# Seven block products in four of 22 pairs of the down products, x scaled in the first gate pass, sums ahead of any split

## The chip, the cores and the metric

The kernel runs on one core of one Trainium2 chip. The metric is the device time of one execution in microseconds (us), from start to end on that core. Engines are named as in the profile: PE is TensorE's matmul, PEld its weight load, DVE is VectorE, ACT is ScalarE, POOL is GpSimd, SP is SyncE (here it only issues DMAs).

## The reference

One decoder layer on x of 256 rows and 2048 columns, float32:

```python
x = x + 0.5 * swiglu(rms_norm(x, g1), gate1, up1, down1)      # D_FF = 5632
x = x + mix(rms_norm(x, g2))   # joint projection, RWKV-7 time mixing | RG-LRU, output projection
x = x + 0.5 * swiglu(rms_norm(x, g3), gate2, up2, down2)
out = rms_norm(x, final_norm)

def rms_norm(x, g): return x * rsqrt(mean(x * x, -1) + 1e-6) * g
def swiglu(x, w_gate, w_up, w_down): return (silu(x @ w_gate) * (x @ w_up)) @ w_down
```

## The kernel before

**Splits.** A float32 operand is split into a high part (a cast to fp32r on ACT, `whi`) and a low part (the difference, on DVE, `wlo`). A product of 128 rows by 512 columns over one k tile of 128 is three matmuls: high by high, high by low, low by high. Weights arrive by DMA from SP, 1 MB (two k tiles of 1024 columns, a *pair*) in one transfer, into `wst`; `wst`, `whi` and `wlo` are three rotating buffers each.

**FFN.** `ffn` walks the 5632 hidden columns in a first chunk of 512 and five of 1024. Each chunk has a gate pass and an up pass over the 16 k tiles of x. In the first chunk x is the row-unscaled input: the transposes come before the row norms are known. Its gate pass multiplies as it is; `after_first()` then makes `rstd`, `spread_rstd` (L203 to L206) lays it along the free axis as `rb`, and the silu and `hid` (L351) take `rstd` as a scale. During the up pass of the first chunk `normalised(p)` scales two k tiles of x at a time for all later chunks: add high and low (L279), times `rb` (L280), cast (L281), low part (L282). For the first three pairs it also makes four block sums of x (L286 to L289) and splits them (L291, L292) into `xsums`.

**S pairs.** In the chunks of 1024, a pass is eight pairs by the plan `nSnSnSnn`. An `n` pair is 24 matmuls of 512 columns (two k tiles, two row tiles, two column halves, three products). An `S` pair treats rows, k and columns as 2x2 blocks and makes seven block products instead of eight, so 21 matmuls; for it `pairs` (L107ff) makes three sums of weight blocks on DVE: L125 (1024 columns), L127 and L128 (512 each), and splits b11/b21, b22, t1/t3 and t2/t4. These four splits take four `whi` buffers in turn; an `n` pair takes two. Products that belong to several output blocks gather in four `aux` banks of PSUM, the others in four `own` banks; `shared` (L296 to L304) adds the `aux` banks into `sg` or `hid` after the last S pair, and the loops at L317 and L324 add the `own` banks after the pass.

**Down.** hidden is transposed (`hidden_T`, L263, evicted at L270, L271) into `hThi` and `hTlo`, 44 k tiles. The down product goes through `weights` and `rows_times` (L174, L175, L177): pieces of 1024 columns in FFN1 (two), one of 1024 and two of 512 in FFN2, all with eight products for each pair. L371 adds half of each bank into the residual `h`.

**Order.** The tile scheduler sets each engine's order by priority. Weight loads, splits and sums of a pair are written at a high priority (offset 4000), so they stand ahead of the work around them. Each engine runs its queue in that order. Mix (`Mix`) runs its projections through `columns_times` (L186 to L188), evicts by `rb` into `raw` (L571) and inverts small matrices on DVE (L754, L758, copy L762) at the same time.

Of the kernel before, what the change touches and what calls it, by code (L numbers as in the profile page):

```python
# [21 lines left out]
class Core:
# [80 lines left out]
    def pairs(self, mat, c0, plan):  # L103
# [3 lines left out]
        ns = plan.count("S")  # L107
        ids = {"S": iter(range(ns)), "n": iter(range(ns, self.NK // 2))}
        for kind in plan:
            p = next(ids[kind])  # L110
# [29 lines left out]
    def rows_times_pairs(self, mat, c0, plan, own, aux, xhi, xlo, sums, hooks):  # L140
# [3 lines left out]
        for at, (kind, p, w) in enumerate(self.pairs(mat, c0, plan)):  # L144
# [7 lines left out]
            else:  # L152
                x = lambda k, t: tuple(v[:, 2 * p + k, t * P : (t + 1) * P] for v in (xhi, xlo))
                sm = lambda n: tuple(sums[:, p, h, n * P : (n + 1) * P] for h in range(2))
# [3 lines left out]
                self.three(own[1], sm(3), w["b22"], first, last)  # L158
                self.three(aux[1], sm(0), w["t1"], f, l)
                self.three(aux[3], sm(2), w["t3"], f, l)  # L160
                self.three(aux[2], sm(1), w["t2"], f, l)
# [84 lines left out]
def ffn(core, xhi, xlo, rstd, wg, wu, wd, after_first, after_down, fpool, down, rest, back, head=None):  # L246
# [11 lines left out]
    def hidden_T(c0, w, hid):  # L258
        for j in range(0, w // P, 2):
# [13 lines left out]
            )  # L273

    def normalised(p):

# [6 lines left out]
        if p < NSUM:  # L283
            blk = lambda k, t: tmp[:, k, t * P : (t + 1) * P]
            raw = scrap[:, 1, 512:].rearrange("p (n s) -> p n s", n=4)
            nc.vector.tensor_tensor(raw[:, 0], blk(0, 1), blk(1, 1), ALU.add)  # L286
            nc.vector.tensor_tensor(raw[:, 1], raw[:, 0], blk(0, 0), ALU.subtract)
            nc.vector.tensor_tensor(raw[:, 2], blk(0, 0), blk(0, 1), ALU.subtract)
            nc.vector.tensor_tensor(raw[:, 3], blk(1, 0), raw[:, 1], ALU.subtract)  # L289
            flat = raw.rearrange("p n s -> p (n s)")  # L290
            nc.scalar.copy(sums[:, p, 0, :], flat)  # L291
            nc.vector.tensor_tensor(sums[:, p, 1, :], flat, sums[:, p, 0, :].bitcast(F32), ALU.subtract)  # L292
# [916 lines left out]
```

## Time and profile before

| what | value |
|---|---|
| median of 3 runs | 1953.26 us (1949.84 to 1953.41) |
| the profiled execution | 1948.99 us, of it the span of the trace 1947.3 us |
| granted TensorE clock, mean | 0.994 |
| PE busy | 1907.3 us (98%) |
| DVE busy | 1440.3 us (74%) |
| ACT busy | 985.8 us (51%) |
| DMA | 360.77 MB, mean 185 GB/s |

All durations and starts of rows come from the profiled execution, which was 4.27 us below the median. A matmul's row lasts longer than its turn: matmuls overlap, so the price of one is the distance between starts. A number in brackets at the end of a row is the idle time of the engine just before it, with the instruction that ended it.

### The profile page before, as it was taken

To read this page: it belongs to the slowest core of one execution; us is meant where nothing else is said; L and a number is where in the kernel's file an instruction comes from. 1 tells how busy PE (TensorE), PEld (TensorE's weight loads), DVE (VectorE), ACT (ScalarE), POOL (GpSimd) and SP (SyncE) were. 2 spreads that over 40 slices of the span, in tenths; PEclk is the share of its full clock that TensorE was granted. 3 is DMA by queue.
4 is the path that set the end of the run, shared out by engine and by line. 5 is a ranking of instruction groups with operands and counts; after the bars stand their busy time and mean duration, and the time that the engine had idled before them with its cause. 6 is when DMAs were issued, how large, how long until landed. Compare 5 with 4: busy or idle time off the path is not lost.

```text
span 1947.3 us, 25669 instructions
## 1 busy us (share of the span) xinstructions
PE 1907.3 (98%) x10233; PEld 1589.7 (82%) x10233; DVE 1440.3 (74%) x1822; ACT 985.8 (51%) x1189; POOL 9.9 (1%) x53
## 2 busy tenths in 40 slices
PE   8899999999999999999999999999999999999997
PEld 6678877878888889998899878778888888788886
DVE  5989898888645446876696775899898989844553
ACT  6465555555444335544454555565556555543443
POOL 0000000000000001000000000000000000000000
PEclk9999999999999999999999999999999999999999
DMA  6356555565755556545243456555555655766553
GB/s 238 129 198 214 173 194 195 178 212 190 264 186 204 194 195 207 177 127 163 77 144 115 131 195 215 173 194 182 199 197 198 211 183 184 257 211 193 195 194 129
DMA packets 130032, 360.77 MB, mean 185 GB/s; under 512 B 20879, under 2 KB 23128, under 8 KB 129784
## 3 DMA queue, kind: packets, MB, share of 16 engines
q1 hardware_dynamic: 129592, 358.08, 55.6%
q8 instruction: 80, 1.31, 0.3%
q10 hardware_dynamic: 320, 1.06, 0.1%
q14 instruction: 40, 0.33, 0.0%
HBM read 351.25 MB, written 7.86 MB: 184 GB/s over the span
## 4 chain that ended last, share of the span: by engine, by line
PE 89%; DVE 5%; ACT 3%; issue 2%; DMA 1%; SPq 0%; ACTq 0%; DVEq 0%
PE bank L137 14%; PE bank L136 13%; PE bank L138 13%; PE bank L175 10%; PE bank L177 10%; PE bank L174 10%; PE bank L186 4%; PE bank L188 4%; PE bank L187 4%; ACT whi L99 1%; DVE wlo L82 1%; PE bank L263 1%; DVE wlo L100 1%; PE bank L712 1%; PE bank L640 1%
## 5 line engine op out<-in xcount | busy, mean ns | idle before, releaser
L82 DVE TENSOR_TENSOR wlo<-wst,whi 128x1024 fp32r<-128x1024 f32 (+2 forms) x329 | 398.2, 1212 | 344.6 <-ACT whi L81 343.9
L99 ACT CAST whi<-wst 128x1024 fp32r<-128x1024 f32 (+1 forms) x440 | 430.4, 993 | 364.0 <-PE bank L138 321.9
L81 ACT CAST whi<-wst 128x1024 fp32r<-128x1024 f32 (+2 forms) x329 | 343.2, 1044 | 472.5 <-PE bank L177 335.8
L100 DVE TENSOR_TENSOR wlo<-wst,whi 128x1024 fp32r<-128x1024 f32 (+1 forms) x440 | 493.3, 1147 | 90.9 <-ACT whi L99 85.0
L174 PE MATMUL bank<-whi,hThi 128*128 128x512 f32 x704 | 274.2, 389 | 0.0
L175 PE MATMUL bank<-wlo,hThi 128*128 128x512 f32 x704 | 274.0, 389 | 0.0
L177 PE MATMUL bank<-whi,hTlo 128*128 128x512 f32 x704 | 231.4, 389 | 0.0
L186 PE MATMUL bank<-xahi,whi 128*128 128x256 f32 x688 | 199.1, 290 | 3.2 <-DVE raw L571 3.2
L188 PE MATMUL bank<-xahi,wlo 128*128 128x256 f32 x688 | 197.9, 288 | 0.0
L136 PE MATMUL bank<-whi,xahi 128*128 128x512 f32 x490 | 191.4, 393 | 6.3 <-ACT xahi L281 4.6
L187 PE MATMUL bank<-xalo,whi 128*128 128x256 f32 x688 | 197.3, 287 | 0.0
L137 PE MATMUL bank<-wlo,xahi 128*128 128x512 f32 x490 | 191.5, 391 | 0.6 <-DVE wlo L100 0.6
L136 PE MATMUL bank<-whi,xbhi 128*128 128x512 f32 x490 | 190.2, 391 | 1.9 <-DVE hid L351 1.4
L137 PE MATMUL bank<-wlo,xbhi 128*128 128x512 f32 x490 | 191.1, 390 | 0.6 <-DVE wlo L100 0.6
L138 PE MATMUL bank<-whi,xalo 128*128 128x512 f32 x490 | 191.4, 391 | 0.0
L138 PE MATMUL bank<-whi,xblo 128*128 128x512 f32 x490 | 190.7, 389 | 0.0
L175 PEld LDWEIGHTS bank<-wlo,hThi 128*128 128x128 f32 x704 | 132.2, 188 | 27.4
L177 PEld LDWEIGHTS bank<-whi,hTlo 128*128 128x128 f32 x704 | 132.1, 188 | 27.4
L174 PEld LDWEIGHTS bank<-whi,hThi 128*128 128x128 f32 x704 | 132.2, 188 | 27.1
L186 PEld LDWEIGHTS bank<-xahi,whi 128*128 128x128 f32 x688 | 133.1, 193 | 7.3 <-DVE raw L571 3.6
L188 PEld LDWEIGHTS bank<-xahi,wlo 128*128 128x128 f32 x688 | 132.9, 193 | 1.9 <-issue 1.1
L187 PEld LDWEIGHTS bank<-xalo,whi 128*128 128x128 f32 x688 | 133.1, 194 | 1.2 <-issue 0.2
(298 smaller groups left out, 2557.3 us busy)
## 6 DMA issues: line engine op xcount, KB each, us to landing
wst<-in_ffn_w_up_dram SPq DMA_DIRECT2D x88, 1024.0 KB, 5.0
wst<-in_ffn_w_down_dram SPq DMA_DIRECT2D x88, 1024.0 KB, 4.9
wst<-in_ffn_w_gate_dram SPq DMA_DIRECT2D x87, 1024.0 KB, 5.0
wst<-in_w_in_dram SPq DMA_DIRECT2D x40, 1024.0 KB, 5.0
wst<-in_w_out_dram SPq DMA_DIRECT2D x16, 1024.0 KB, 5.7
h<-parked SPq DMA_DIRECT2D x4, 1024.0 KB, 9.2
wst<-in_w_in_dram SPq DMA_DIRECT2D x4, 640.0 KB, 4.4
h<-in_x_dram SPq DMA_DIRECT2D x4, 512.0 KB, 4.7
```

The lines of the kernel that those rows point to most:

```text
L82: nc.vector.tensor_tensor(lo[:, : m * width], src, hi[:, : m * width].bitcast(F32), ALU.subtract)
L99: self.nc.scalar.copy(hv, src)
L100: self.nc.vector.tensor_tensor(lv, src, hv.bitcast(F32), ALU.subtract)
L136: nc.tensor.matmul(out, a[0], b[0], start=first, stop=False)
L137: nc.tensor.matmul(out, a[0], b[1], start=False, stop=False)
L138: self.last_mm = nc.tensor.matmul(out, a[1], b[0], start=False, stop=last)
L174: nc.tensor.matmul(banks[t][n][:, :w], a, whi[:, c : c + w], start=first, stop=False)
L175: nc.tensor.matmul(banks[t][n][:, :w], a, wlo[:, c : c + w], start=False, stop=False)
L177: self.last_mm = nc.tensor.matmul(banks[t][n][:, :w], b, whi[:, c : c + w], start=False, stop=last)
L186: nc.tensor.matmul(out, a, xhi[:, k, :], start=first, stop=False, skip_group_check=True)
L187: nc.tensor.matmul(out, a, xlo[:, k, :], start=False, stop=False, skip_group_check=True)
L188: nc.tensor.matmul(out, b, xhi[:, k, :], start=False, stop=last, skip_group_check=True)
```

## The change

1. **Down.** Pieces of 1024 columns go through `rows_times_pairs` with 22 pairs, four of them S (the last eight k tiles, at positions 6, 10, 14, 18 of the first piece and 3, 8, 13, 18 of the second; FFN2 has only a first piece). `hidden_T` of the last chunk comes after pair 2; it makes the block sums of the hidden tiles too. `shared_h` adds the `aux` banks into `h` after the last S pair.
2. **x scaled earlier.** `after_first()` and `normalised` move into the gate pass of the first chunk: after the seventh k tile in FFN1, after the first in FFN2. The up pass reads scaled x and makes the block sums; `hid` needs no `rstd`. The S pairs of x are now pairs 1, 3 and 5.
3. **Sums first.** In an S pair the three sums stand ahead of the four splits, and b22's split has a buffer of its own, so that an S pair takes three rotating buffers instead of four.
4. **Mix.** The evictions by `rb` are written at offset 3900; one reciprocal of 1024 columns is cut in four. x and its low part lie in two half tiles each; a junk tile moves to another pool.

```diff
     def split(self, src, n):
-        hi = self.wpool.tile([P, self.WMAX], F32R, name=self.name("whi"), tag="whi")
-        lo = self.wpool.tile([P, self.WMAX], F32R, name=self.name("wlo"), tag="wlo")
+        pool = self.wpool if n == 2 else self.bpool
+        hi = pool.tile([P, n * 512], F32R, name=self.name("whi"), tag="whi" if n == 2 else "whb")
+        lo = pool.tile([P, n * 512], F32R, name=self.name("wlo"), tag="wlo" if n == 2 else "wlb")
...
-                    b11, b21 = self.split(b[:, :, 0, :], 2)
-                    (b22,) = self.split(b[:, 1, 1:2, :], 1)
                     nc.vector.tensor_tensor(t[:, 0:2], b[:, :, 1, :], b[:, 0], ALU.subtract)
-                    t1, t3 = self.split(t[:, 0:2], 2)
                     nc.vector.tensor_tensor(t[:, 2], t[:, 1], b[:, 0, 0, :], ALU.add)
                     nc.vector.tensor_tensor(t[:, 3], b[:, 1, 0, :], t[:, 2], ALU.subtract)
+                    b11, b21 = self.split(b[:, :, 0, :], 2)
+                    (b22,) = self.split(b[:, 1, 1:2, :], 1)
+                    t1, t3 = self.split(t[:, 0:2], 2)
                     t2, t4 = self.split(t[:, 2:4], 2)
...
+    def block_sums(r, hi, lo):
+        blk = lambda k, t: r[:, k, t * P : (t + 1) * P]
+        nc.vector.tensor_tensor(blk(1, 1), blk(0, 1), blk(1, 1), ALU.add)
+        nc.vector.tensor_tensor(blk(0, 1), blk(0, 0), blk(0, 1), ALU.subtract)
+        nc.vector.tensor_tensor(blk(0, 0), blk(1, 1), blk(0, 0), ALU.subtract)
+        nc.vector.tensor_tensor(blk(1, 0), blk(1, 0), blk(0, 0), ALU.subtract)
+        flat = r.rearrange("p k s -> p (k s)")
+        nc.scalar.copy(hi, flat)
+        nc.vector.tensor_tensor(lo, flat, hi.bitcast(F32), ALU.subtract)
...
+    def shared_h(aux, tmp, c0):
+        t1, t2, t3, _ = blocks_of(tmp)
+        nc.scalar.copy(t1, aux[0])
+        nc.vector.tensor_tensor(t2, aux[2], t1, ALU.add)
+        nc.vector.tensor_tensor(t3, aux[3], t2, ALU.add)
+        for (t, n), parts in (((0, 1), (aux[1], t2)), ((1, 0), (t3,)), ((1, 1), (aux[1], t3)), ((0, 0), (t1,))):
+            hs = core.h[:, t, c0 + n * 512 : c0 + (n + 1) * 512]
+            for part in parts:
+                nc.vector.scalar_tensor_tensor(hs, part, 0.5, hs, ALU.mult, ALU.add)
...
+        norm_at, scaled = 6 if head else 0, 0
         for i, (k, hi, lo) in enumerate(core.weights([(wg, c0, w)], ks, head=bool(head))):
             core.rows_times(gb, xhi, xlo, k, hi, lo, w, i == 0, i == NK - 1)
...
-        after_first()
+            if i == norm_at:
+                after_first()
...
+            if i % 2 and i >= norm_at:
+                while scaled <= i // 2:
+                    normalised(scaled)
+                    scaled += 1
...
         for i, (k, hi, lo) in enumerate(core.weights([(wu, c0, w)], ks)):
             core.rows_times(ub, xhi, xlo, k, hi, lo, w, i == 0, i == NK - 1)
-            if i % 2:
-                normalised(i // 2)
+            if i % 2 and i // 2 in place:
+                block_sums(room(i // 2), *sums(place[i // 2]))
...
+        if w == 1024:
+            plan = DOWN_PLAN[piece]
+            number = {"n": iter(range(first_s)), "S": iter(range(first_s, NF // 2))}
+            ids = [next(number[kind]) for kind in plan]
...
+            hooks[plan.rindex("S")] = [lambda: shared_h(aux, tmp(), c0)]
+            core.rows_times_pairs(wd, c0, plan, ids, own, aux, hT_hi, hT_lo, hsums, hooks)
...
+            with self.tc.high_priority(offset=3900):
+                nc.vector.tensor_tensor(
+                    raw[:, :n, 1:257], bk[:, : n * 256].rearrange("p (a s) -> p a s", a=n),
...
+DOWN_PLAN, DOWN_HIDDEN_AT = ("nnnnnnSnnnSnnnSnnnSnnn", "nnnSnnnnSnnnnSnnnnSnnn"), 2
```

Three places show what this moves on DVE. First, an S pair with the `n` pair ahead of it in a steady gate pass. Before (L100 is the low part of a split; `wst_247` holds the sums of S weights in `wst_242`, and `wst_237` the n pair):

```order
L100 TENSOR_TENSOR wlo_239_1383<-wst_237_1380,whi_238_1382 128x1024
L100 TENSOR_TENSOR wlo_241_1387<-wst_237_1380,whi_240_1386 128x1024
L125 TENSOR_TENSOR wst_247_1424<-wst_242_1414 128x1024
L100 TENSOR_TENSOR wlo_244_1417<-wst_242_1414,whi_243_1416 128x1024
L127 TENSOR_TENSOR wst_247_1424<-wst_247_1424,wst_242_1414 128x512
L100 TENSOR_TENSOR wlo_246_1421<-wst_242_1414,whi_245_1420 128x512
L128 TENSOR_TENSOR wst_247_1424<-wst_242_1414,wst_247_1424 128x512
L100 TENSOR_TENSOR wlo_249_1427<-wst_247_1424,whi_248_1426 128x1024
L100 TENSOR_TENSOR wlo_251_1433<-wst_247_1424,whi_250_1432 128x1024
```

After (L116 is the low part, L136 to L138 the sums; `wst_249` holds the sums of `wst_248`, `wst_243` the n pair):

```order
L116 TENSOR_TENSOR wlo_245_1386<-wst_243_1383,whi_244_1385 128x1024
L136 TENSOR_TENSOR wst_249_1419<-wst_248_1417 128x1024
L116 TENSOR_TENSOR wlo_247_1390<-wst_243_1383,whi_246_1389 128x1024
L137 TENSOR_TENSOR wst_249_1419<-wst_249_1419,wst_248_1417 128x512
L116 TENSOR_TENSOR wlo_251_1424<-wst_248_1417,whi_250_1423 128x1024
L138 TENSOR_TENSOR wst_249_1419<-wst_248_1417,wst_249_1419 128x512
L116 TENSOR_TENSOR wlo_253_1428<-wst_248_1417,whi_252_1427 128x512
L116 TENSOR_TENSOR wlo_255_1432<-wst_249_1419,whi_254_1431 128x1024
L116 TENSOR_TENSOR wlo_257_1436<-wst_249_1419,whi_256_1435 128x1024
```

The first sum now stands ahead of the second low part of the n pair, the third sum ahead of b22's low part, and t1/t3 no longer stand between n and the sums.

Second, DVE from the spreading of `rstd` in FFN1's first chunk. Before (L82 is the low part of a weight tile, L1071 a copy of gains):

```order
L206 COPY rb_41_354<-bank_40_349 128x256
L1071 COPY gT_80<-bank_42_358 128x16
L82 TENSOR_TENSOR wlo_56_433<-wst_52_426,whi_55_432 128x1024
L1071 COPY gT_80<-bank_43_363 128x16
L279 TENSOR_TENSOR sg_44_366<-xahi_101,xalo_102 128x512
L82 TENSOR_TENSOR wlo_59_477<-wst_57_474,whi_58_476 128x1024
L280 TENSOR_TENSOR sg_44_366<-sg_44_366,rb_41_354 128x512
L286 TENSOR_TENSOR sg_44_366<-sg_44_366 128x128
L288 TENSOR_TENSOR sg_44_366<-sg_44_366 128x128
L287 TENSOR_TENSOR sg_44_366<-sg_44_366 128x128
L289 TENSOR_TENSOR sg_44_366<-sg_44_366 128x128
L82 TENSOR_TENSOR wlo_61_481<-wst_57_474,whi_60_480 128x1024
```

After (L97 is the low part of a weight tile, L312, L313 and L315 the add, the scaling and the low part of x):

```order
L219 COPY rb_37_283<-bank_36_278 128x256
L313 TENSOR_TENSOR hid_41_296<-hid_41_296,rb_37_283 128x512
L1134 COPY gT_80<-bank_38_287 128x16
L313 TENSOR_TENSOR hid_41_296<-hid_41_296,rb_37_283 128x512
L97 TENSOR_TENSOR wlo_56_411<-wst_54_408,whi_55_410 128x1024
L315 TENSOR_TENSOR xalo_3_102<-hid_41_296,xahi_1_100 128x512
L315 TENSOR_TENSOR xalo_4_103<-hid_41_296,xahi_2_101 128x512
L312 TENSOR_TENSOR hid_41_296<-xahi_1_100,xalo_3_102 128x512
L97 TENSOR_TENSOR wlo_58_415<-wst_54_408,whi_57_414 128x1024
L1134 COPY gT_80<-bank_39_292 128x16
L312 TENSOR_TENSOR sg_40_295<-xahi_1_100,xalo_3_102 128x512
L313 TENSOR_TENSOR hid_41_296<-hid_41_296,rb_37_283 128x512
```

Before, one pair of x is scaled with its block sums between the weights of the up pass; now three pairs are taken up between the weights of the gate pass, without their sums.

Third, DVE in mix at the end of one matrix inversion. Before (L754, L758 and L762 are the inversion, L571 the evictions that free two banks):

```order
L758 TENSOR_TENSOR inv_1083_6545<-inv_1083_6545,invw_1084_6546 64x28x3
L754 TENSOR_TENSOR invw_1084_6546<-inv_1083_6545 64x58
L758 TENSOR_TENSOR inv_1083_6545<-inv_1083_6545,invw_1084_6546 64x29x2
L754 TENSOR_TENSOR invw_1084_6546<-inv_1083_6545 64x30
L758 TENSOR_TENSOR inv_1083_6545<-inv_1083_6545,invw_1084_6546 64x30
L762 COPY invw_1084_6546<-inv_1083_6545 64x1024
L82 TENSOR_TENSOR wlo_1204_7559<-wst_1200_7552,whi_1203_7558 128x1024
L571 TENSOR_TENSOR raw_1147_7172<-bank_1124_6937,rb_969_5528 128x2x256
L571 TENSOR_TENSOR raw_1148_7179<-bank_1125_6938,rb_969_5528 128x2x256
```

After (L813, L817 and L821 are the inversion, L629 the evictions):

```order
L97 TENSOR_TENSOR wlo_1269_7699<-wst_1265_7692,whi_1268_7698 128x1024
L813 TENSOR_TENSOR invw_1149_6686<-inv_1148_6685 64x84
L629 TENSOR_TENSOR raw_1212_7312<-bank_1189_7077,rb_1034_5668 128x2x256
L629 TENSOR_TENSOR raw_1213_7319<-bank_1190_7078,rb_1034_5668 128x2x256
L817 TENSOR_TENSOR inv_1148_6685<-inv_1148_6685,invw_1149_6686 64x28x3
L818 MEMSET inv_1148_6685 64x32
L813 TENSOR_TENSOR invw_1149_6686<-inv_1148_6685 64x58
L97 TENSOR_TENSOR wlo_1272_7753<-wst_1270_7750,whi_1271_7752 128x1024
L817 TENSOR_TENSOR inv_1148_6685<-inv_1148_6685,invw_1149_6686 64x29x2
```

The two evictions moved from behind the copy and a weight's low part to ahead of the last steps of the inversion.

## Rows read from the trace of the kernel before

**Rows 1.** The page: span, busy time of the engines, and the chain by engine.

```profile
span 1947.3 us, 25669 instructions
...
PE 1907.3 (98%) x10233; PEld 1589.7 (82%) x10233; DVE 1440.3 (74%) x1822; ACT 985.8 (51%) x1189; POOL 9.9 (1%) x53
...
PE 89%; DVE 5%; ACT 3%; issue 2%; DMA 1%; SPq 0%; ACTq 0%; DVEq 0%
```

**Rows 2.** Windows: start:end, length, busy us (x) PE, PEld, DVE, ACT, POOL; PEclk, DMA, GB/s.

```profile
25.00:50.00 25.00, 24.38 (x108) 19.40 (x107) 14.66 (x23) 17.10 (x23) 0.00 (x0) 1.00 0.59 199
50.00:75.00 25.00, 18.18 (x73) 14.05 (x72) 23.27 (x38) 10.37 (x14) 0.00 (x0) 0.86 0.27 85
650.00:700.00 50.00, 50.00 (x222) 41.41 (x221) 22.89 (x19) 18.99 (x18) 0.00 (x0) 1.00 0.58 197
1250.00:1275.00 25.00, 22.31 (x93) 16.74 (x92) 23.37 (x32) 12.64 (x15) 0.00 (x0) 1.00 0.33 116
193.31:453.72 260.41, 259.62 (x1148) 208.64 (x1147) 230.90 (x259) 144.44 (x162) 0.00 (x0) 1.00 0.59 194
```

**Rows 3.** Timeline, PE, end of FFN1's first up pass: start us, us, engine, line, operation.

```profile
60.28 0.39 PE L177 MATMUL bank<-whi,xalo 128*128 128x512 f32 x1
...
60.96 0.39 PE L177 MATMUL bank<-whi,xalo 128*128 128x512 f32 x1
...
69.38 0.80 PE L136 MATMUL bank<-whi,xahi 128*128 128x512 f32 x1 [4.56 <-ACT xahi L281]
...
70.82 0.63 PE L136 MATMUL bank<-whi,xahi 128*128 128x512 f32 x1
71.25 0.63 PE L137 MATMUL bank<-wlo,xahi 128*128 128x512 f32 x1
```

**Rows 4.** Timeline, DVE, from the spread rstd to the first scaling of x in FFN1.

```profile
40.34 0.42 DVE L206 COPY rb<-bank 128x256 f32<-128x256 f32 x1
...
45.16 0.68 DVE L279 TENSOR_TENSOR sg<-xahi,xalo 128x512 f32<-128x512 f32 x1
```

**Rows 5.** Timelines, DVE and PE, FFN2's start: rstd, its spread, the first stall after it.

```profile
1223.12 0.47 DVE L203 TENSOR_SCALAR rdiag<-ident,rstd 128x128 f32<-128x128 f32 x2
...
1236.87 0.42 DVE L206 COPY rb<-bank 128x256 f32<-128x256 f32 x1 [0.86 <-PE bank L204]
...
1260.02 0.47 PE L136 MATMUL bank<-whi,xbhi 128*128 128x512 f32 x1 [1.38 <-DVE hid L351]
```

**Rows 6.** Timelines, PE and DVE, an S pair inside a steady gate pass.

```profile
218.39 0.61 PE L136 MATMUL bank<-whi,xsums 128*128 128x512 f32 x2
...
219.25 0.39 PE L138 MATMUL bank<-whi,xsums 128*128 128x512 f32 x1
...
210.92 1.22 DVE L125 TENSOR_TENSOR wst<-wst 128x1024 f32<-128x1024 f32 x1
...
215.09 0.69 DVE L127 TENSOR_TENSOR wst<-wst,wst 128x512 f32<-128x512 f32 x1
```

**Rows 7.** Chain of waits of one pass: transposes of a hidden chunk, and a weight load.

```profile
269.01 6.73 DMA wst<-in_ffn_w_gate_dram
...
281.26 1.09 PE bank L263 x8
```

**Rows 8.** The page: splits' groups (busy, mean ns), and a weight load's median us to landing.

```profile
L100 DVE TENSOR_TENSOR wlo<-wst,whi 128x1024 fp32r<-128x1024 f32 (+1 forms) x440 | 493.3, 1147 | 90.9 <-ACT whi L99 85.0
...
wst<-in_ffn_w_gate_dram SPq DMA_DIRECT2D x87, 1024.0 KB, 5.0
```

**Rows 9.** Timelines, DVE and PE, the wait in the mix stage.

```profile
883.80 1.03 DVE L762 COPY invw<-inv 64x1024 f32<-64x1024 f32 x1
884.75 1.21 DVE L82 TENSOR_TENSOR wlo<-wst,whi 128x1024 fp32r<-128x1024 f32 x1
885.89 1.27 DVE L571 TENSOR_TENSOR raw<-bank,rb 128x512 f32<-128x512 f32 x2
...
886.62 0.39 PE L186 MATMUL bank<-xahi,whi 128*128 128x256 f32 x1 [3.05 <-DVE raw L571]
```

More of the change, by code (lines that the diff above doesn't have):

```diff
@@ L19, with __init__, __getitem__ @@
 EPS = 1e-6
+class Halves:
+    def __init__(self, *tiles):
+        self.tiles = list(tiles)
+    def __getitem__(self, at):
+        rows, k, cols = at
+        if isinstance(k, slice):
+            i, k = k.start // 8, slice(k.start % 8, k.start % 8 + k.stop - k.start)
+        else:
+            i, k = k // 8, k % 8
+        return self.tiles[i][rows, k, cols]
 class Core:
@@ L101, in split, with pairs @@
         return [(hi[:, i * 512 : i * 512 + 512], lo[:, i * 512 : i * 512 + 512]) for i in range(n)]
-    def pairs(self, mat, c0, plan):
+    def pairs(self, mat, c0, plan, ids):
         nc = self.nc
[L107 to L110, printed above, removed]
+        for kind, p in zip(plan, ids):
             with self.tc.high_priority(offset=4000):
@@ L138, in three, with rows_times_pairs @@
         self.last_mm = nc.tensor.matmul(out, a[1], b[0], start=False, stop=last)
-    def rows_times_pairs(self, mat, c0, plan, own, aux, xhi, xlo, sums, hooks):
+    def rows_times_pairs(self, mat, c0, plan, ids, own, aux, xhi, xlo, sums, hooks):
         ns, done = plan.count("S"), 0
-        for at, (kind, p, w) in enumerate(self.pairs(mat, c0, plan)):
+        for at, (kind, p, w) in enumerate(self.pairs(mat, c0, plan, ids)):
             first, last = at == 0, at == len(plan) - 1
@@ L157, in rows_times_pairs @@
                 self.three(aux[0], x(0, 0), w["b11"], f, l)
[L158 to L161, printed above, removed]
+                self.three(own[1], sm(4), w["b22"], first, last)
+                self.three(aux[1], sm(1), w["t1"], f, l)
+                self.three(aux[3], sm(3), w["t3"], f, l)
+                self.three(aux[2], sm(2), w["t2"], f, l)
                 self.three(own[2], x(1, 1), w["t4"], first, last)
@@ L243, in rstd_of, with ffn @@
         nc.vector.reciprocal(rstd, tmp)
-def ffn(core, xhi, xlo, rstd, wg, wu, wd, after_first, after_down, fpool, down, rest, back, head=None):
+def ffn(core, xhi, xlo, rstd, wg, wu, wd, after_first, after_down, fpool, down, rest, back, spare, head=None):
     nc, NT, NK, D, S = core.nc, core.NT, core.NK, core.D, core.S
@@ L282, in normalised, with room @@
         nc.vector.tensor_tensor(xlo[:, pair, :], tmp, xhi[:, pair, :].bitcast(F32), ALU.subtract)
[L283 to L292, printed above, removed]
+    def room(p):
+        at = place.get(p, 3)
+        return (scrap, hid)[at // 2][:, at % 2, 512:].rearrange("p (k s) -> p k s", k=2)
     def blocks_of(dst):
@@ L314, in ffn @@
             hooks.setdefault(HIDDEN_AT, []).extend(pending)
-            core.rows_times_pairs(wg, c0, GATE_PLAN, own, aux, xhi, xlo, sums, hooks)
+            core.rows_times_pairs(wg, c0, GATE_PLAN, ids, own, aux, xhi, xlo, lambda p: sums(place[p]), hooks)
             for d, bk in zip(blocks_of(sg), own):
@@ L920, in lru @@
         nc.vector.tensor_scalar(D, T1, -1.0, -1.0, ALU.mult, ALU.add)
-        nc.vector.reciprocal(D, D)
+        for j in range(4):
+            nc.vector.reciprocal(D[:, j * 256 : (j + 1) * 256], D[:, j * 256 : (j + 1) * 256])
         nc.vector.scalar_tensor_tensor(XC, TI, 1.0, XC, ALU.add, ALU.mult)
@@ L1084, in xt_pool, with half, sums @@
         pool = stack.enter_context(tc.tile_pool(name=name, bufs=1, **kw))
-        return [pool.tile([P, NK, S], F32R, name=name + n) for n in ("hi", "lo")]
+        def half(n, i):
+            return pool.tile([P, NK // 2, S], F32R, name=core.name(name + n), tag=f"{n}{i}")
+        def sums():
+            tiles = [pool.tile([P, 4, 512], F32R, name=core.name(name + "sum"), tag=f"{n}1") for n in ("hi", "lo")]
+            return lambda p: tuple(t[:, p % 4, :] for t in tiles)
+        return [Halves(half(n, 0), half(n, 1)) for n in ("hi", "lo")], half, sums
     with ExitStack() as front:
-        xa = xt_pool(front, "xa")
+        xa, xa_half, xa_sums = xt_pool(front, "xa")
         with ExitStack() as st:
@@ L1159, in closing @@
             c0, w = down[piece]
[L1160 removed]
+            core.sumsq(c0, w, ssq[3][piece], fpool)
             for t in range(core.NT):
```

109 lines of the change are left out of this document (63 added, 46 removed).

## The prediction

> **What bounds the kernel now.** I read the page first: PE is busy 98% of the span and holds 89% of the chain that ended last, DVE 74% of the time, ACT 51% [rows 1]. So the time is the number of matmuls times their turn, plus the places where PE stands. The turn is read next, from starts: 60.28 to 60.96 is three matmuls, 0.227 us each [rows 3], though each row is 0.39 long; the down window has 222 matmuls in 50 us, 111 in 25 [rows 2]. Then I went along the span in windows of 25 us and looked for fewer than 111 matmuls at 512 columns. Two windows stand out: 50 to 75 has 73, and 1250 to 1275 has 93 [rows 2]. These are 38 and 18 turns short, 8.6 and 4.1 us. In both, DVE is busy over 23 of 25 us, while in 25 to 50 it was busy 14.66 of 25 [rows 2]: x is scaled in a hurry in the up pass, behind weights that cannot wait. The stall is seen at 69.38, where PE had waited 4.56 us for a cast of x; after it the starts at 70.82 and 71.25 are 0.43 apart, and the window's granted clock is 0.86, so part of it ran at 1.2 GHz instead of 2.4 [rows 2, 3]. Third are the steady chunks: 260.41 us for three chunks [rows 2]. Each has 2 x (5 x 24 + 3 x 21) = 366 matmuls, 83.0 us, and 16 transposes at 0.136 (eight took 1.09 [rows 7]), 2.2 us: 85.2 of 86.8, so 1.65 us per chunk is lost. It is in the S pairs: from 218.39 to 219.25 three turns took 0.86 instead of 0.68 [rows 6]. Last, mix has one wait of 3.05 us, for an eviction that stood behind a copy and a low part on DVE [rows 9].
>
> **Fewer matmuls in the down products.** Three pieces of 1024 columns with four S pairs each, three matmuls fewer per S: 36 x 0.227 = 8.2 us off PE, all on the path since PE has no idle time there (50.00 of 50.00 busy [rows 2]). What is added lies beside it. For each piece, DVE gets per S pair 1.22 + 2 x 0.69 us of sums [rows 6] and low parts of 3.5 x 1.15 instead of 2 x 1.15 us [rows 8], 4.3 us in all; eight more operations of 512 columns (0.69 each) come with the `aux` banks; the block sums of the hidden tiles are some 20 small ones, once per FFN. That is about 17.3 + 5.5 us per piece, and DVE is busy only 22.89 of 50 us there [rows 2], in a piece that lasts about 118 us. If a cover fails, the nearest price is an S pair's loss in the steady chunks, 1.65 / 6 = 0.27 us, so 12 x 0.27 = 3.3 us at most; the other end is nothing. I take 0.5, near nothing, because DVE and ACT have twice the room that they have in the gate and up passes. A gain below nothing is not possible, as PE does not wait there now. Term: -8.2 + 0.5.
>
> The Trainium skill bears on the size: its page "TensorE: Matmul & The Clock Gate", section "Back-to-back issue gap", gives about 131 ns for sustained matmuls of 512 columns and about 216 for isolated ones. The rows' 227 ns are near the isolated figure although these matmuls come in an unbroken stream; by the page's sustained figure 36 matmuls would be 4.7 us, an estimate, and the total 3.5 us less good. The trace decides here.
>
> **x scaled in the first gate pass.** In FFN1, `rb` is there at 40.34 but the first scaling starts at 45.16 [rows 4], and the work ends in the stall at 69.38. DVE idles 10.3 us of the window ahead [rows 2]. The move takes three pairs into that idle time, then the rest one by one; the up pass keeps only the block sums of three pairs. I followed both queues by hand with these durations: DVE is full from about 31 us on; the up pass reaches the second pair of x at about 42.0, and its low part is ready at about 44.5, because two low parts of weights stand ahead of it. So 2.3 us of wait come back (the nearest rows for its ends: 0 and the 4.56 of now), and the old stall goes, since after the scaling DVE needs only its 1.15 us per weight tile [rows 8] and small sums. Term: 8.6 - 2.3 = -6.3, between -8.6 and +1 (the wait as long as now, with the low clock behind it again).
>
> In FFN2, `rstd`'s diagonal is made at 1223.12 but spread only at 1236.87, because the two small matmuls of the spreading stand behind the gate pass; the first stall is at 1260.02 [rows 5]. Now the spreading is inside the gate pass, a dozen us earlier, and all scaling can be over before the up pass is half through. PE may wait some 0.4 us at the diagonal (its duration, 0.47 [rows 5]). Term: 4.1 - 0.4 = -3.7, between -4.1 and 0. The scaling adds nothing to the count of DVE's operations; each is made once, before or after.
>
> **Sums first, and b22's own buffer.** Before, t2/t4 take the buffer that b11/b21 left, so ACT's cast waits for PE to use b11, in the same S pair that needs t2 a few turns later. With three buffers instead of four, t2/t4 take one that the n pair before has left: free at the start of S, 15 turns or 3.4 us ahead of t2, against a cast and a low part, about 1 and 1.15 us [rows 8]. I expect the S pair's waits to go. What comes in is one wait: `aux` banks of a pass are the `own` banks of the last one, and an eviction of these now stands behind a low part on DVE; I make it 0.45 us in the first S of a gate pass, and leave 0.2 for the rest. 1.65 - 0.65 = 1.0 per chunk, for nine chunks (the first of each FFN is half in the term above): -9. Ends: 0, if the wait only moves, and -15, nine times 1.65.
>
> **Mix.** The evictions pass the copy (1.03) and the low part (1.21) [rows 9] and the last inversion steps, so most of the 3.05 goes: -3, between 0 (the inversion ends later by as much, and its own user waits) and -5 (with some of the other waits on evictions, all shorter). The rest of the change (tiles, pools, a reciprocal in four) has no row on the path: nothing, 0.3 either way.
>
> **Sum.** -7.7 - 6.3 - 3.7 - 9 - 3 = -29.7. The profiled execution took 1948.99, which gives 1919.3; the median of the runs is 4.27 above it, so I say 1923.5.
>
> **Rivals.**
> The load loop, on the other side. The first sum of S now stands ahead of the n pair's second low part, and it waits for the S pair's weights. These are loaded when the S pair before has let go of its buffer, after b22's low part. The loop: landing 5.0 [rows 8], sum 1.15, low part 1.15, sum 0.6, low part 1.15, sum 0.6, low part of b22 0.6 (half of b11's): 10.25 us, against 45 turns or 10.2 us of PE for an n and an S pair. It just holds; b22 is needed six turns into S, which leaves some 0.4. Each us of landing beyond that comes back in the second and third S pair of 20 passes, 40 us for each us. The median is 5.0; the chain has one load of 6.73 [rows 7]. If all were so: 40 x 1.3 = 52 and no gain of 9 in the S pairs, so 1953.3 - 20.7 + 52 = 1985. It decides against the change from a landing of about 5.9 on. Against it: the median, and that the first S of a pass starts with two n pairs of lead. Chance 0.04.
>
> The clock, on the same side. After the stall in FFN1 the turns were 0.43 us [rows 3], and at that level (1.2 GHz) an S pair costs 21 x (0.43 - 0.227) = 4.3 us more. If the down's S pairs waited often enough to bring it down, 12 of them would cost 51 us: 1975. The steady chunks speak against it: six S pairs in each, with such short waits, and a granted clock of 1.00 over 260 us [rows 2]. Chance 0.01. The Trainium skill has such a rule, which speaks against this change: on the same page, the section "A second HAM failure mode: psum-queue depth-cycling" says that short idles between groups of matmuls can bring the array to half clock again and again. The trace does not bear it out for these pairs [rows 2].
>
> The scaling's wait only moves: DVE's total in the first chunk is the same, and if the wait in the up pass is over 4 us and takes the clock down, FFN1 gives nothing: 1930. Chance 0.12.
>
> The S pairs' waits stay, because ACT or the weights and not the buffer end them: 1932.5, with FFN2's term half gone up to 1935. Chance 0.14.
>
> Only the count tells, all waits come back elsewhere: 1953.3 - 8.2 = 1945. Chance 0.05.
>
> **How the numbers follow.** The forecast, with its terms' smaller errors (1914 to 1931), has 0.64. The range 1913 to 1936 holds it and the two rivals that lose one term, 0.90 less the edges, about 0.82. About 0.2% or 4 us is what a measurement of this kernel can tell from no change. Faster: all but the first two rivals and some mixtures, 0.93; the same 0.03; slower 0.04.
>
> **What would show it.** The down windows should keep 111 matmuls in 25 us. The windows that answer to 50 to 75 and 1250 to 1275 should have over 100 matmuls and a clock near 1.00; a wait of 2 to 3 us for a low part of x should stand near 42 us. Three steady chunks should take about 257.5 us, with no wait on t2/t4's cast and the first S of a gate pass waiting for an eviction. The 3.05 in mix should be under 0.5. I am wrong if the sums of S begin late behind landings, if the clock falls near 45 us, or if down windows have gaps.

## The result and the profile after

The changed kernel takes 1919.3 us (median of 4 runs, 1917.9 to 1919.58) against 1952.19 us for the kernel before on the same chip; the ratio is 0.9831 (95% interval 0.9814 to 0.9849), 33 us less. Forecast were 1923.5 us and a range of 1913 to 1936.

The page of the changed kernel, as [rows 1]: span, busy time, chain by engine.

```profile
span 1917.7 us, 25761 instructions
...
PE 1885.3 (98%) x10197; PEld 1591.7 (83%) x10197; DVE 1513.9 (79%) x1952; ACT 1012.8 (53%) x1232; POOL 9.9 (1%) x53
...
PE 83%; DVE 10%; DMA 4%; ACT 1%; issue 1%; SPq 0%; DVEq 0%; ACTq 0%
```

PE is as full as before with 36 matmuls fewer; DVE has gone from 74% to 79% and from 5% to 10% of the chain. Windows of the changed kernel, as [rows 2] (bounds and length; busy us and count of PE, PEld, DVE, ACT, POOL; granted clock, DMA share, GB/s); the stages begin a little earlier than before, and the windows are moved with them:

```profile
25.00:50.00 25.00, 22.85 (x101) 18.06 (x100) 21.55 (x38) 17.49 (x23) 0.00 (x0) 1.00 0.60 201
50.00:75.00 25.00, 25.00 (x111) 20.48 (x111) 23.82 (x34) 14.43 (x18) 0.00 (x0) 1.00 0.38 127
640.00:690.00 50.00, 50.00 (x222) 41.42 (x221) 31.49 (x29) 23.24 (x23) 0.00 (x0) 1.00 0.56 196
1215.00:1240.00 25.00, 25.00 (x112) 20.69 (x111) 25.00 (x40) 17.91 (x24) 0.00 (x0) 1.00 0.52 168
1240.00:1265.00 25.00, 24.95 (x110) 20.34 (x109) 22.13 (x27) 13.56 (x15) 0.00 (x0) 1.00 0.54 170
193.00:448.00 255.00, 254.42 (x1141) 209.60 (x1140) 230.37 (x258) 143.48 (x162) 0.00 (x0) 1.00 0.58 198
```

The window from 50 to 75 has 111 matmuls (73 before) at a clock of 1.00, the start of FFN2 112 and 110 (93 before), the down window 222, as before, while DVE works 31.49 us there instead of 22.89. The time by stage, from the first matmul of one to the first of the next (both profiled executions):

| stage | before, us | after, us | change |
|---|---|---|---|
| FFN1 gate and up | 495.55 | 483.84 | -11.7 |
| FFN1 down | 243.11 | 237.68 | -5.4 |
| mix | 466.26 | 466.63 | +0.4 |
| FFN2 gate and up | 482.09 | 471.32 | -10.8 |
| FFN2 down | 240.90 | 238.21 | -2.7 |
| ahead of the first and behind the last matmul | 19.4 | 20.0 | +0.6 |

Inside the gate and up stages the way from the first matmul to the first transposes of hidden went from 99.79 to 93.26 us in FFN1 and from 86.87 to 82.54 in FFN2 (-10.9 together); the steady chunks from 86.5 to 85.4 (FFN1) and from 86.4 to 85.0 (FFN2), and with what follows them they make the other -11.6.

### The profile page after: what moved, and what is told of

It reads as the page before. It is cut to its first block, busy times and chain, and to the rows that moved or that the text cites. A ratio compares the mean times of both kernels' runs of the same rounds, so it can differ in the third digit from the quotient of the medians.

```text
span 1917.7 us, 25761 instructions
## 1 busy us (share of the span) xinstructions
PE 1885.3 (98%) x10197; PEld 1591.7 (83%) x10197; DVE 1513.9 (79%) x1952; ACT 1012.8 (53%) x1232; POOL 9.9 (1%) x53
## 4 chain that ended last, share of the span: by engine, by line
PE 83%; DVE 10%; DMA 4%; ACT 1%; issue 1%; SPq 0%; DVEq 0%; ACTq 0%
PE bank L149 17%; PE bank L151 17%; PE bank L150 17%; PE bank L190 5%; PE bank L188 5%; PE bank L187 4%; PE bank L200 4%; PE bank L199 4%; PE bank L201 4%; DVE wlo L116 3%; DMA wst<-in_ffn_w_gate_dram 3%; DVE wlo L97 1%; PE bank L280 1%; PE bank L771 1%; PE bank L699 1%
## 5 line engine op out<-in xcount | busy, mean ns | idle before, releaser
L115 ACT CAST whi<-wst 128x1024 fp32r<-128x1024 f32 (+1 forms) x596 | 589.0, 1001 | 542.7 <-PE bank L151 484.8
L116 DVE TENSOR_TENSOR wlo<-wst,whi 128x1024 fp32r<-128x1024 f32 (+1 forms) x596 | 682.6, 1156 | 146.0 <-ACT whi L115 136.9
L97 DVE TENSOR_TENSOR wlo<-wst,whi 128x1024 fp32r<-128x1024 f32 (+2 forms) x197 | 236.7, 1203 | 150.6 <-ACT whi L96 149.5
L96 ACT CAST whi<-wst 128x1024 fp32r<-128x1024 f32 (+2 forms) x197 | 204.1, 1037 | 258.0 <-PE bank L190 115.7
L149 PE MATMUL bank<-whi,hThi 128*128 128x512 f32 x468 | 182.5, 390 | 0.0
L151 PE MATMUL bank<-whi,hTlo 128*128 128x512 f32 x468 | 182.2, 389 | 0.0
L150 PE MATMUL bank<-wlo,hThi 128*128 128x512 f32 x468 | 182.1, 389 | 0.0
L136 DVE TENSOR_TENSOR wst<-wst 128x1024 f32<-128x1024 f32 x72 | 88.1, 1223 | 28.8 <-DMA wst<-in_ffn_w_up_dram 10.5
L149 PEld LDWEIGHTS bank<-whi,xahi 128*128 128x128 f32 x490 | 92.0, 188 | 20.3 <-PE bank L151 0.8
L149 PEld LDWEIGHTS bank<-whi,xbhi 128*128 128x128 f32 x490 | 92.0, 188 | 19.8 <-PE bank L151 0.8
```

The lines of the kernel that those rows point to most:

```text
L96: self.last_split = nc.scalar.copy(hi[:, : m * width], src)
L97: nc.vector.tensor_tensor(lo[:, : m * width], src, hi[:, : m * width].bitcast(F32), ALU.subtract)
L115: self.nc.scalar.copy(hv, src)
L116: self.nc.vector.tensor_tensor(lv, src, hv.bitcast(F32), ALU.subtract)
L149: nc.tensor.matmul(out, a[0], b[0], start=first, stop=False)
L150: nc.tensor.matmul(out, a[0], b[1], start=False, stop=False)
```

## The experiments

Edits of e1 to e5 and e7 to e12 are against the changed kernel, e6 against the kernel before. Stage times are of the profiled execution of each kernel.

**The down products, e1.** All pairs are n pairs:

```diff
-        if w == 1024:
+        if False:
             own, aux = ...
```

> The changed kernel with all 22 pairs of the down products as n pairs (eight products each), and no block sums of the hidden tiles. Theory: the S pairs in the down cost nothing beside their matmuls, so 36 matmuls of 0.227 us come back: +8.2 us against the changed kernel (1919.3), 1927.5, and the three pieces of 1024 columns get 2.72 us longer each. Rival: the S pairs have some cost of their own (waits, aux evictions), then less than +8.2 comes back; at 0.27 us of wait per S pair +5.

1931.0 us (1929.5 to 1938.0), +11.7. The two down stages got 243.11 and 240.90 us again, the very numbers of the kernel before: 8.12 us for 36 matmuls, 0.2256 each. So the S pairs in the down cost nothing beside their matmuls, and the first theory holds for these stages. The other 3.6 us of the median lie elsewhere: in the profiled execution mix (472.67) and FFN2's gate and up (476.38), which the edit does not touch, are longer. (That execution took 1938.0, above all its others, so its stages overstate this; in mix the low clock cost it 10.2 us instead of 5.1, counted as under e5.) In FFN2 the first sum of an S pair waited longer for its weights; waits of DVE in four steady chunks of FFN2 (us in total, times, longest), e1 first, then the changed kernel:

```profile
DVE wst L136 <- DMA wst<-in_ffn_w_gate_dram: 9.0, 8, 2.0
DVE wst L136 <- DMA wst<-in_ffn_w_up_dram: 5.3, 8, 1.2
```

```profile
DVE wst L136 <- DMA wst<-in_ffn_w_gate_dram: 4.3, 8, 0.8
DVE wst L136 <- DMA wst<-in_ffn_w_up_dram: 4.2, 7, 1.0
```

Whether these loads started later or took longer to land is not settled.

**b22's buffer, e2.**

```diff
-        pool = self.wpool if n == 2 else self.bpool
-        hi = pool.tile([P, n * 512], F32R, name=self.name("whi"), tag="whi" if n == 2 else "whb")
+        hi = self.wpool.tile([P, self.WMAX], F32R, name=self.name("whi"), tag="whi")
```

> The changed kernel with b22's split back in the three rotating buffers; the sums still stand ahead of all splits. Theory: the buffer of its own is what took the S pairs' waits away; they come back, 1.65 us in each of ten chunks: +10 to +16 us, 1929 to 1935, and a steady chunk goes from 85.0 to about 86.6 us. Rival: the order of the sums did it; then within 2 us of 1919.3.

1933.5 us (1932.3 to 1936.7), +14.2; steady chunks of 85.7 to 86.9 us. The stall is the old one: in an S pair of the down, three turns from 637.12 to 637.98 took 0.86 us, as from 218.39 to 219.25 in [rows 6]. Timeline of PE in e2:

```profile
637.12 0.61 PE L148 MATMUL bank<-whi,xasum 128*128 128x512 f32 x2
637.65 0.50 PE L149 MATMUL bank<-wlo,xasum 128*128 128x512 f32 x1
637.98 0.39 PE L150 MATMUL bank<-whi,xasum 128*128 128x512 f32 x1
```

It is priced twice more: FFN1's down is 2.19 us longer with eight such pairs, FFN2's 1.07 with four, 0.27 us each, the price that the prediction gave for a cover that fails.

**The order of sums and splits, e3.**

```diff
+                    b11, b21 = self.split(b[:, :, 0, :], 2)
+                    (b22,) = self.split(b[:, 1, 1:2, :], 1)
                     nc.vector.tensor_tensor(t[:, 0:2], b[:, :, 1, :], b[:, 0], ALU.subtract)
+                    t1, t3 = self.split(t[:, 0:2], 2)
                     nc.vector.tensor_tensor(t[:, 2], t[:, 1], b[:, 0, 0, :], ALU.add)
                     nc.vector.tensor_tensor(t[:, 3], b[:, 1, 0, :], t[:, 2], ALU.subtract)
-                    b11, b21 = self.split(b[:, :, 0, :], 2)
-                    (b22,) = self.split(b[:, 1, 1:2, :], 1)
-                    t1, t3 = self.split(t[:, 0:2], 2)
```

> The changed kernel with sums and splits of an S pair in the order of the kernel before (b11/b21, b22, first sum, t1/t3, the other sums, t2/t4); b22 keeps its own buffer. Theory (the buffer counts): within 2 us of 1919.3, 1918 to 1921, steady chunks 85.0 to 85.2. Rival (the order counts): +10 to +16 us, chunks of 86.6.

1920.1 us (1916.5 to 1920.4): nothing. "Sums ahead of any split" is worth no time here; the buffer is.

**The buffer alone, e6**, in the kernel before:

```diff
+        pool = self.wpool if n == 2 else self.bpool
+        hi = pool.tile([P, n * 512], F32R, name=self.name("whi"), tag="whi" if n == 2 else "whb")
...
+        junk = pool.tile([P, w], F32, name=self.name("junk"), tag="hid")
```

> The kernel before with one thing of the change: b22's split has its own buffer (a junk tile gives the room for it); sums, scaling, down and mix as before. Theory: the S pairs' waits go, 1.65 us in each of ten chunks less some new wait: -9 to -13 us against the kernel before (1952.2), 1939 to 1943, with steady chunks of 85.0 to 85.6 us. Rival (order): within 2 us of 1952.2, chunks of 86.6.

1943.3 us (1941.6 to 1946.7), ratio 0.9959 (0.9944 to 0.9973), 8 us less, a little short of the 9 to 13 expected. FFN1's steady chunks went to 84.8 to 85.6, FFN2's only to 85.0, 85.7, 86.4 and 86.8: the gate and up stage is 5.7 us shorter in FFN1 and 1.1 in FFN2. In FFN2's steady chunks PE waited three times for a low part, 1.5 us together, which it does not in the changed kernel; what makes this difference is not settled. The stalls at the start of the FFNs are untouched: first transposes after 99.92 and 87.94 us.

**Where x is scaled, e4.** `after_first()` behind the gate pass, `normalised` in the up pass:

```diff
         for i, (k, hi, lo) in enumerate(core.weights([(wu, c0, w)], ks)):
             core.rows_times(ub, xhi, xlo, k, hi, lo, w, i == 0, i == NK - 1)
+            if i % 2:
+                normalised(i // 2)
             if i % 2 and i // 2 in place:
                 block_sums(room(i // 2), *sums(place[i // 2]))
```

> The changed kernel with x scaled during the first up pass again, as in the kernel before. Theory: the stalls at the start of both FFNs come back, 8.6 + 4.1 us less the 2.3 of wait that the changed kernel has there: +10.4 us, 1929.7, with a stall of 4 to 5 us and a half clock near 65 us. Rival: b22's buffer and the sums' order had already eased DVE at that place, so that only some 3 to 5 us come back, 1922 to 1924.

1920.2 us (1918.9 to 1922.8): only 0.9 us came back. Both theories miss. The gate and up stages are 0.5 and 0.4 us longer; the first transposes come after 95.44 and 83.07 us. From 42 us to the first transposes of FFN1 PE is left with two short waits, for casts of weights; timeline of PE in e4:

```profile
73.32 1.20 PE L149 MATMUL bank<-whi,xahi 128*128 128x512 f32 x4 [1.13 <-ACT whi L115]
...
77.83 1.43 PE L149 MATMUL bank<-whi,xahi 128*128 128x512 f32 x5 [1.13 <-ACT whi L115]
```

**The pairs of x that S takes, e9 and e10.** e4 and the changed kernel with the old pairs:

```diff
-    ids = range(NK // 2)
-    place = {p: n for n, p in enumerate(p for p in ids if "S" in (GATE_PLAN[p], UP_PLAN[p]))}
+    ids = [3, 0, 4, 1, 5, 2, 6, 7]
+    place = {0: 0, 1: 1, 2: 2}
```

> The kernel that scales x in the first up pass (e4_scale_up), with the S pairs on pairs 0, 1 and 2 of x and the first n pair on pair 3, as in the kernel before. Theory: what ended the stalls at the start of the FFNs is that the pairs of x are now used in the order in which they are scaled, and not the place of the scaling; with the old pairs the stall of 4 to 5 us with half clock near 65 us is back: from the start to the first transposes 99.8 us instead of 95.4, in FFN2 86.9 instead of 83.1, in all +8 us against e4_scale_up, about 1928. Rival: b22's buffer and the sums' order ended them: within 2 us of 1920.2.

> The changed kernel, x scaled in the first gate pass, with the S pairs on pairs 0, 1 and 2 of x and the first n pair on pair 3. Theory: once all pairs are scaled before the first chunk of 1024 begins, their order does not matter: within 2 us of 1919.3, first transposes 93.3 us after the start. Rival: the order matters by itself: +4 to +8 us, 1923 to 1927.

e9: 1919.2 us (1918.7 to 1919.7), first transposes after 90.67 and 81.90 us. The pairing is not the cause either. e10: 1921.3 us (1919.0 to 1925.3), within what was expected.

In e10 the first transposes come after 95.00 us instead of the 93.3 expected. One profiled execution does not fix such numbers to better than some 2 us: in e11, the changed kernel once more, it is 91.32 us against 93.26, and the clock's fall at 21.54 us of the one is not in the other.

What e4 and e9 still share with the changed kernel, and e6 does not, is the room for scaled x (`room`: four temporary places of 512 columns instead of one and a second for the block sums), x in half tiles, and the sums first. The multiplications by `rb` on DVE show what differs. The first three in the kernel before, whose up pass ends at 61 us:

```profile
46.90 0.68 DVE L280 TENSOR_TENSOR sg<-sg,rb 128x512 f32<-128x512 f32 x1
...
52.96 0.68 DVE L280 TENSOR_TENSOR sg<-sg,rb 128x512 f32<-128x512 f32 x1
...
63.94 0.68 DVE L280 TENSOR_TENSOR sg<-sg,rb 128x512 f32<-128x512 f32 x1
```

The first five in e9, which scales in the same pass:

```profile
40.91 0.69 DVE L313 TENSOR_TENSOR hid<-hid,rb 128x512 f32<-128x512 f32 x1
...
41.60 0.69 DVE L313 TENSOR_TENSOR hid<-hid,rb 128x512 f32<-128x512 f32 x1
...
46.23 0.69 DVE L313 TENSOR_TENSOR sg<-sg,rb 128x512 f32<-128x512 f32 x1
...
47.56 0.69 DVE L313 TENSOR_TENSOR sg<-sg,rb 128x512 f32<-128x512 f32 x1
...
64.64 0.69 DVE L313 TENSOR_TENSOR hid<-hid,rb 128x512 f32<-128x512 f32 x1
```

`rb` is ready at 40.34 before and at 40.45 in e9. By 48 us e9 has begun four pairs, the kernel before one; with one temporary place a pair must be cast and subtracted before the next one may be added. FFN2 has the same: from `rb` on (1236.87 before, 1221.15 in e9) the kernel before has multiplied one pair in the first 5 us, e9 four. Before, then e9:

```profile
1237.33 0.69 DVE L280 TENSOR_TENSOR sg<-sg,rb 128x512 f32<-128x512 f32 x1
...
1243.37 0.69 DVE L280 TENSOR_TENSOR sg<-sg,rb 128x512 f32<-128x512 f32 x1
```

```profile
1221.61 1.29 DVE L313 TENSOR_TENSOR sg<-sg,rb 128x512 f32<-128x512 f32 x2
...
1222.82 0.68 DVE L313 TENSOR_TENSOR hid<-hid,rb 128x512 f32<-128x512 f32 x1
...
1225.16 0.68 DVE L313 TENSOR_TENSOR hid<-hid,rb 128x512 f32<-128x512 f32 x1
```

e6 shows this chain, one pair behind the other (L283 add, L286 low part, which frees the place), and the stalls of PE at its end:

```profile
61.68 0.69 DVE L283 TENSOR_TENSOR sg<-xahi,xalo 128x512 f32<-128x512 f32 x1
...
64.88 0.69 DVE L286 TENSOR_TENSOR xalo<-sg,xahi 128x512 fp32r<-128x512 f32 x1
...
66.75 0.69 DVE L283 TENSOR_TENSOR sg<-xahi,xalo 128x512 f32<-128x512 f32 x1
...
69.33 0.69 DVE L286 TENSOR_TENSOR xalo<-sg,xahi 128x512 fp32r<-128x512 f32 x1 [0.69 <-ACT xahi L285]
```

```profile
64.92 0.77 PE L137 MATMUL bank<-whi,xahi 128*128 128x512 f32 x1 [4.25 <-DVE hid L355]
...
69.35 0.80 PE L137 MATMUL bank<-whi,xahi 128*128 128x512 f32 x1 [2.81 <-ACT xahi L285]
```

So the place in which x is scaled matters little, and the number of pairs that can be under way is what the traces point to. That edit alone was not run; half tiles and, with late scaling, the order of sums are not excluded.

**Mix, e5 and e12** (the same kernel twice), beside e11, the changed kernel once more:

```diff
-            with self.tc.high_priority(offset=3900):
+            with ExitStack():
```

> The changed kernel with the evictions of mix at their old priority. Theory: DVE is full in the stretch of mix that waits (48.74 of 50 us in the changed kernel), so the order of its work there moves no time: the mix stage stays within 0.7 us of its 466.6, the time within 1 of 1919.3. Rival (the prediction's term was right, and something else in mix took the gain back): the stage gets 3 us longer, 1922.5.

> The changed kernel once more, as the base of the next run: 1917.9 to 1919.6, median about 1919.

> The changed kernel with the evictions of mix at their old priority, once more. Theory: its 3.7 us of advantage are half of them the clock in mix, which fell less often in its profiled run (3.4 us lost to the low clock instead of 5.2) and falls by chance: within 2 us of the changed kernel run beside it. Rival: the priority costs 3 to 4 us: 1915.5, and the profiled run again loses under 4 us to the low clock in mix.

e5: 1915.6 us (1913.8 to 1918.8). e11: 1919.7 us (1917.6 to 1923.5), ratio 0.9837 (0.9823 to 0.9851). e12: 1914.3 us (1912.1 to 1917.6), ratio 0.9806 (0.9793 to 0.9820). Without the priority the median is 3.7 us (e5) and, beside e11, 5.4 us (e12) lower, and this version beats both kernels. Both my theories fall, that nothing moves and that it is chance, and e12's rival holds. The clock shows a part of why. Adding up (1 - granted clock) over mix gives 3.4 us in e5 and e12, in the kernel before and in e6, which have no priority, and 5.1 to 10.2 in all ten kernels that have it (5.1 in the changed kernel, 6.8 in e11). The stage itself takes 465.07 and 465.53 us in e5 and e12, 466.63 in the changed kernel, 467.69 in e11, and 470.47 and 472.67 in e10 and e1, which lost 10.2 to the clock. So the traces have 1.6 and 2.2 us of the 3.7 and 5.4 in mix; the rest lies in other stages and in executions that were not traced. In the ten kernels one window of 20 us about 300 us into mix has 0.74 to 0.85, in the other four it has 1.00. In the changed kernel it looks so; timeline of PE, then two windows of 4 us:

```profile
1024.19 2.21 PE L839 MATMUL bank<-inv,gram 32*32 32x32 f32 x64
...
1026.99 2.63 PE L843 MATMUL bank<-gram,inv 32*32 32x32 f32 x64
...
1029.94 0.41 PE L199 MATMUL bank<-xahi,whi 128*128 128x256 f32 x1
1030.15 0.41 PE L200 MATMUL bank<-xalo,whi 128*128 128x256 f32 x1
```

```profile
1025.06:1029.06 4.00, 4.00 (x104) 3.83 (x101) 3.96 (x3) 1.78 (x4) 0.00 (x0) 0.93 0.26 97
1029.06:1033.06 4.00, 4.00 (x27) 3.94 (x26) 0.04 (x1) 2.12 (x4) 0.00 (x0) 0.50 0.00 0
```

Two groups of 64 small matmuls (32x32) run from 1024.19 and 1026.99, with four large ones between them. PE does not idle (4.00 of 4.00 busy), but the clock falls at 1028.47, within the second group, and the turns are 0.21 us from 1029.94 on instead of 0.12, the level of 1.2 GHz. In e12 the same groups start 6.2 us apart, with some 18 large matmuls and another group between them, and the clock stays at 1.00:

```profile
1025.37 2.21 PE L839 MATMUL bank<-inv,gram 32*32 32x32 f32 x64
...
1029.75 1.89 PE L1008 MATMUL bank<-gate,ones 128*128 128x256 f32 x8
1031.57 2.21 PE L843 MATMUL bank<-gram,inv 32*32 32x32 f32 x64
```

```profile
1030.07:1034.07 4.00, 4.00 (x78) 3.50 (x77) 0.42 (x1) 2.38 (x5) 0.00 (x0) 1.00 0.78 254
```

The same two groups come once earlier in mix (900.34 and 903.14 in the changed kernel). There they start 2.8 us apart in all fourteen kernels, the kernel before and e12 too, and each time the clock falls. At the second place they start 2.8 us apart in nine of the ten kernels with the priority, and the clock falls; 4.2 us apart in the kernel before and in e6, 6.2 in e5 and e12, and it does not. In e1 they start 3.9 us apart, and the clock fell before the second began, so how close the two stand is not all of it. No run moved these groups alone.

The Trainium skill ("TensorE: Matmul & The Clock Gate", section "HAM oscillation — how this bites in real kernels") puts such falls down to idle gaps between bursts of matmuls; here the clock fell with PE busy throughout (4.00 of 4.00 us above), on small matmuls.

**The load loop, e7.** A second, small load (64 columns of one k tile, 32 KB) behind that of each S pair of gate and up:

```diff
+                if kind == "S" and self.NK == mat.shape[0] // P:
+                    nc.sync.dma_start(out=st[:, 0:RELOAD], in_=mat[2 * p * P : (2 * p + 1) * P, c0 : c0 + RELOAD])
```

> The changed kernel, where the weights of each S pair of the gate and up passes are followed by a second load of 64 of their columns for 128 rows into the same place, so that the first sum must wait for one more landing. Theory of the load loop: what is added to the landing beyond some 0.4 us comes back in the second and third S pair of the 20 passes, 40 us for each us; with about 2 us added, some 60 us: 1980 (1955 to 2000). Rival: the loop has several us of room; then below +8 us, 1927 or less.

1930.9 us (1927.4 to 1932.2), +11.6. The chain of waits in e7 gives the landing that was added, 1.78 us behind a load of 5.02:

```profile
296.75 5.02 DMA wst<-in_ffn_w_up_dram
301.76 0.02 issue
301.78 1.78 DMA wst<-in_ffn_w_up_dram
```

The time lies between the theory's 1955 to 2000 and the rival's 1927. It is 6.5 us for each us of landing, or, at the prediction's 40 us for each us beyond the room of the loop, a room of 1.5 us and not 0.4; one run cannot tell these apart. Either way the loop has more room than I gave it. One reservation: with the second load the scheduler put the first sum behind the second low part of the n pair again, which itself widens the loop.

**More S pairs, e8.** Four in each pass (the fourth's sums are made from another pair of x):

```diff
-GATE_PLAN, UP_PLAN, NSUM = "nSnSnSnn", "nSnSnSnn", 3
-HIDDEN_AT = 6
+GATE_PLAN, UP_PLAN, NSUM = "nSnSSnSn", "nSnSSnSn", 4
+HIDDEN_AT = 7
```

> The changed kernel with four S pairs in each pass of the gate and up products (plan nSnSSnSn, sums for four pairs of x). It saves three matmuls in each of 20 passes, 60 x 0.227 = 13.6 us. Theory: DVE gets 4.0 us more per chunk, where it already works about 77 of 85 us, and two S pairs in a row ask 12.6 us of DVE in 9.5 us of PE: the waits take back most or all, between -5 and +25 us against 1919.3. Rival: only the count tells, -13.6, 1905.7.

1975.9 us (1972.6 to 1979.6), 56.6 more, far beyond my bound. Steady chunks take 89 to 92 us instead of 85. A window of e8's steady chunks:

```profile
195.00:460.00 265.00, 252.36 (x1079) 199.95 (x1080) 243.98 (x278) 145.51 (x165) 0.00 (x0) 0.98 0.54 182
```

DVE is at 92% (90% in the changed kernel) and PE at 95%. PE waited in this window 7.1 us for the additions into `sg`, 4.1 us for casts and 2.0 us for low parts, and the clock fell once in each steady chunk. Each S pair asks about 6.3 us of DVE in 4.8 us of PE, and I read the waits as two in a row leaving nothing to catch up with before the bank evictions; a plan of four that keeps them apart was not run.

## Why the prediction was right, and where its steps were not

The time and the sum were right (-29.7 us forecast on the profiled execution, -29.6 measured from 1948.99 to 1919.43), the reasons only in part.

**Fewer matmuls in the down: right.** -7.7 forecast (8.2 less 0.5 for waits), -8.12 measured, at 0.2256 us a turn and with no wait added. By the 131 ns that the Trainium skill ("TensorE: Matmul & The Clock Gate", section "Back-to-back issue gap") gives for sustained matmuls of 512 columns it would have been 4.7 us, an estimate; the trace does not bear it out for these.

**Start of the FFNs: right in size, wrong in its cause.** -6.3 and -3.7 forecast, -6.5 and -4.3 measured (-8.5 and -4.4 in e11), and even the wait that comes back was there, forecast as 2.3 us near 44.5. Timeline of PE in the changed kernel:

```profile
46.29 0.73 PE L190 MATMUL bank<-whi,xalo 128*128 128x512 f32 x2 [2.15 <-DVE xalo L315]
```

But the step that gave the gain to the move into the gate pass failed. e4 undid the move and lost 0.9 us, and e9, without the move and with the old pairs, is as fast as the changed kernel. What gave the gain in its place stays open: the traces point to the four places for scaled x, and no run has these alone. I read the diff as a move of work into DVE's idle time, and passed over that the same lines gave the scaling four places instead of one. The old trace had the sign of it, the 0.68 us that DVE idled for ACT's cast in the middle of the hurry:

```profile
69.36 0.69 DVE L282 TENSOR_TENSOR xalo<-sg,xahi 128x512 fp32r<-128x512 f32 x1 [0.68 <-ACT xahi L281]
```

I had followed DVE's order and not asked why the pairs stood one behind the other in it.

**b22's buffer: right, and too small.** -9 forecast, -11.6 measured over these chunks; e2 and e6 bear out the mechanism, e3 that the order has no part in it beside the buffer. The buffer alone gave 8 in e6, nearly all of it in FFN1; taking it out cost 14.2 in e2. The term was mis-sized by the 0.65 us of waits that I left in each chunk, most of it in the first S of each gate pass: steady chunks take 85.0 us in FFN2, less than the 85.2 of matmuls and transposes that I counted, so next to nothing is left to wait for. (86.8 less 85.2 is 1.6 and not 1.65; that is 0.5 us over nine chunks.)

**Mix: wrong.** -3 forecast, +0.4 measured. The evictions did move ahead, and PE waited 2.61 us all the same instead of the 3.05 of [rows 9]. DVE, then PE, in the changed kernel:

```profile
867.22 1.21 DVE L97 TENSOR_TENSOR wlo<-wst,whi 128x1024 fp32r<-128x1024 f32 x1
868.35 0.23 DVE L813 TENSOR_TENSOR invw<-inv 64x84 f32<-64x84 f32 x1
868.51 1.27 DVE L629 TENSOR_TENSOR raw<-bank,rb 128x512 f32<-128x512 f32 x2
```

```profile
869.24 0.39 PE L199 MATMUL bank<-xahi,whi 128*128 128x256 f32 x1 [2.61 <-DVE raw L629]
```

Without the priority it is the same, timeline of PE in e5:

```profile
868.39 0.58 PE L199 MATMUL bank<-xahi,whi 128*128 128x256 f32 x1 [2.64 <-DVE raw L629]
```

The eviction starts 139.59 us into mix in the kernel before, 139.44 in the changed kernel and 139.31 in e5. The inversion's copy, ahead of it at 137.50 before, is behind it at 143.73 and, in e5, at 142.91: it was passed without the priority too, and nothing was won. The step that failed is that a place in the order was worth its copy and low part. DVE worked 48.77 of the 50 us from 834 to 884, so I read it as fallen behind, with the eviction late by the work ahead of it, whichever that was. And with the priority the clock fell once more, behind small matmuls close together on PE: 3.4 us of lost clock by itself, 1.7 more over mix than in the kernel before, which I had in no term.

**The rivals.** The load loop did not decide; its room was too small or its price too high, as e7 shows, and the 0.4 us of room is not worked out in the prediction (the six turns that it names are 1.36 us). Still, longer waits on landings are what e1's trace has in FFN2. The clock did fall, not in the down but in mix. That the sum came out to 0.1 us is luck: the buffer's chunks gave 2.6 us more, the starts 0.9 and the down 0.4, mix 3.4 less, and the ends grew by 0.6.

## What to carry to other kernels

Where PE waits on a split, count the turns of the rotating buffers before reordering the work: one small buffer of its own for the odd piece was worth 8 to 14 us here, the order nothing. Where a chain of small steps runs one item behind the other, ask how many places its temporary has; the traces of e6 and e9 point to this, and no run shows it alone. Judge a priority by what it does to the engine at the end of the chain: here it cost some 4 to 5 us, with small matmuls bunched on PE.
